# Gate transposes behind the second and third projections, copied by ScalarE; the weight sums' transfers on GpSimd's own queue

## The chip, the cores and the metric

The kernel runs on one core of a Trainium2 chip. The metric is the time of one execution in device microseconds; lower is better. "The profiled execution" is one execution taken by the hardware profiler.

## The reference

One decoder block over 1024 tokens of width 1024, float32. After a root mean square norm, one product with `w_in` gives the inputs of two parallel token mixers: RWKV-7 (r, k, v and three low-rank inputs) and an mLSTM (q, k, v, o and two gates a head). Their outputs go through `w_out`; then comes a gated ConvFFN.

```python
h = rmsnorm(x, norm1_g[l]);  proj = h @ w_in[l]
y_rw = rwkv7_group(p_rw, ...);  y_ml = mlstm_group(p_ml, ...)
x = x + jnp.concatenate([y_rw, y_ml], axis=-1) @ w_out[l]
u = rmsnorm(x, norm2_g[l]) @ w_ffn_up[l];  a, b = u[..., :D_FF], u[..., D_FF:]
x = x + (jax.nn.silu(causal_dwconv(a, ...)) * b) @ w_ffn_down[l]

# mlstm_group, gates of four heads and 1024 tokens
ig = softcap((ig + i_bias).astype(jnp.float32))
logf = jax.nn.log_sigmoid(softcap((fg + f_bias).astype(jnp.float32)))
# in mlstm_chunkwise: b = cumsum(fc), running maxima m_t, and
# h = num / max(|den|, exp(-m_t)), chunk by chunk with a carried state
```

## The kernel before

Tokens lie along the free dimension. Each float32 product is three fp32r matmuls of high and low parts (`mm3`, L211 to L214). The order of the work is written in the program, but a scheduler under it sets each engine's queue and gives tiles of one tag to buffers; a tile that takes a used buffer waits for every user of the tile before it. The tag `slab` has four such buffers.

The stretch of interest begins behind the norm and the mLSTM's value projection (`vgates`). `gates()` turns the gate inputs `gtm` (tokens on partitions) into rows: eight transposes for the input gate and eight for the forget gate (L392), four copies out of PSUM (L394) into the rows `igr` and `lfr` of a `slab` tile (`slab_797`), two scans (L395, L396), differences and exponentials into the rows of a second one (`slab_798`), transposes back (L417), and two copies into `tcol` (L419), which every mLSTM chunk reads.

Then the projections run in the order q0, q1, mk0, mk1, lo, g, r0 to r3, k0 to k3, v0 to v3. `project()` makes two halves of 512 tokens, each 24 matmuls of 128x512. Their weights come by SP's queue (L218); ScalarE casts the high half (L200), GpSimd subtracts the low half (L201). q and mk pass a causal convolution into another `slab` tile (`do_qk`, L460 to L490). The mLSTM's eight chunks run as generators that one `tick()` in each projection advances: scores (L512, L514), values (L532, L537), state (L550, L557), key transposes (L519, L521), normalization (L541 to L565) and the transposes back (L569).

Beside all this, sums and differences of the blocks of `w_down`, needed only by the last product, are made in eleven jobs, each of two 512 KB loads (L306), two subtractions on VectorE (L311, L313) and two on GpSimd (L312, L314), and one 1 MB store (L317). They share one `slab` tile (`slab_671`) used as a ring of two. Before, loads and stores are issued by SP, in one queue with the projections' weights. `next(weight_sums)` and `spawn(weight_sums)` set where they stand.

Of the kernel before, what the change touches and what calls it, by code (L numbers as in the profile page):

```python
# [17 lines left out]
P = 128  # L18
# [55 lines left out]
def block_kernel(ctx, tc, x, wp, wv, pc, rows, brow, lnrow, wud, wug, w_out, wup, w_down, cst, out):  # L74
    nc = tc.nc
    MM = nc.tensor.matmul
    V = nc.vector
    S = nc.scalar
    G = nc.gpsimd
    dma = nc.sync.dma_start  # L80
# [100 lines left out]
    HF = [slice(0, HALF), slice(HALF, T)]  # L181
# [15 lines left out]
    d_w = dram.tile([NP, P, 4, HALF], F32, name="d_w")  # L197
# [99 lines left out]
    wsums = {}  # L297
    ws_slab = []

    def ws_load(p):  # L300

        if not ws_slab:
            ws_slab.append(slab([P, 2, 4, HALF]))
        wsums[p] = b = ws_slab[0][:, p % 2]
        for q in range(2):
            dma(out=b[:, 2 * q:2 * q + 2], in_=w_down[(2 * p + q) * P:(2 * p + q + 1) * P, :].rearrange("p (h t) -> p h t", h=2))  # L306

    def ws_sum(p):

# [4 lines left out]
        G.tensor_tensor(out=b21, in0=b21, in1=b22, op=ALU.subtract)  # L314

    def ws_store(p):
        dma(out=d_w[p], in_=wsums.pop(p))  # L317

    def ws_jobs():

# [41 lines left out]
    tcol = tmp.tile([P, NT, 4, 4], F32, name="tcol")  # L362

    def gates():
# [20 lines left out]
        V.tensor_tensor(out=ga[:, 0, :], in0=ga[:, 0, :], in1=ga[:, 1, :], op=ALU.mult)  # L385
        V.tensor_tensor(out=ga[:, 0, :], in0=ga[:, 0, :], in1=ga[:, 2, :], op=ALU.mult)
        V.scalar_tensor_tensor(out=yf, in0=yf, scalar=0.0, in1=ga[:, 0, :], op0=ALU.min, op1=ALU.subtract)
        for g, dst in ((0, igr), (1, lfr)):
            for hf in range(2):
                ps = bank(3)  # L390
                for t_ in range(4):
                    nc.tensor.transpose(out=ps[0:4, t_ * P:(t_ + 1) * P], in_=gtm[:, g, 4 * hf + t_, :],  # L392
                                        identity=ident)
                V.tensor_copy(out=dst[:, HF[hf]], in_=ps[0:4, :])  # L394
        V.tensor_tensor_scan(out=mr, data0=lfr, data1=igr, initial=0.0, op0=ALU.add, op1=ALU.max)  # L395
        V.tensor_tensor_scan(out=br, data0=rm128, data1=lfr, initial=0.0, op0=ALU.mult, op1=ALU.add)  # L396
        V.tensor_tensor(out=st[0:4, :], in0=igr, in1=br, op=ALU.subtract)
# [13 lines left out]
        V.tensor_tensor(out=lf3, in0=st3[0:4], in1=al3[:, :, P - 1:P].broadcast_to([4, NT, P]), op=ALU.add)  # L411
        S.activation(out=st[64:68, :], in_=lfr, func=AF.Exp)
        S.activation(out=st[96:100, :], in_=mr, func=AF.Exp, scale=-1.0)
        for hf in range(2):
            ps = bank(3)
            for t_ in range(4):
                nc.tensor.transpose(out=ps[:, t_ * P:(t_ + 1) * P], in_=st[:, (4 * hf + t_) * P:(4 * hf + t_ + 1) * P],  # L417
                                    identity=ident)
            V.tensor_copy(out=tcol[:, 4 * hf:4 * hf + 4],  # L419
                          in_=ps.rearrange("p (c q r) -> p c q r", c=4, q=4)[:, :, :, 0:4])  # L420


    active = []
# [21 lines left out]
    def project(name):  # L445
        w = pweights(name)
        ps = [phalf(w, 0, 1)]
        tick()
        ps.append(phalf(w, 1, 2))
        return ps  # L450
# [323 lines left out]
    def do_v2(p, ts):  # L774
# [8 lines left out]
                    in_=t_o.rearrange("p (c e v) -> p e c v", c=4, e=2)[:, e])  # L783
        yield 1

    gates()
    spawn(weight_sums)
    for name in ORDER[:-IN_CHAIN]:
        i = int(name[-1]) if name[-1].isdigit() else 0
        if name[0] == "k":  # L790
            do_k(i)
        else:
            ps = project(name)
            if name[0] == "q":
                do_qk(i, ps)
            elif name[0] == "m":
                do_qk(2 + i, ps)
                if i == 1:
                    spawn(mlstms())
            elif name[0] == "o":  # L800
                for hf in range(2):
                    do_o(i, hf, ps[hf], t2("vt"), t2("lnb"))
            elif name == "lo":
                do_lo(ps)
            elif name == "g":
                do_g(ps)
            elif name[0] == "r":
                do_r(i, ps)
            else:
                do_v(i, ps)  # L810
        tick()
# [469 lines left out]
    with tc.tile_pool(name="ff", bufs=1) as ff:  # L1281
# [182 lines left out]
        for f in range(1, 3):  # L1464
            r = raw_up(f)
# [203 lines left out]
```

## Time and profile before

| | us |
|---|---|
| median of three runs | 1375.9 |
| the three runs | 1374.04, 1375.9, 4844.43 |
| profiled execution | 1363.99 |
| its span | 1362.2 |
| PE busy in the span | 1273.2 (93%) |
| DVE, ACT, POOL busy | 1008.4, 525.0, 508.5 |
| mean granted clock | 0.963 |

A row of a timeline gives an instruction's start, its length, and in brackets the idle time of its engine just before it with what ended that. Matmuls overlap in the pipeline, so a matmul's length is more than the step from one to the next. PEclk 1.00 in a window is TensorE's full clock of 2.4 GHz, 0.50 is 1.2 GHz.

### The profile page before, as it was taken

The page shows a single profiled execution, that of the slowest core. Times are in us where ns is not written, and L with a number is a line of the kernel's source. Part 1 is how long each engine was busy: PE and PEld are TensorE (multiplying, and loading weights), DVE is VectorE, ACT ScalarE, POOL GpSimd, SP SyncE. Part 2 cuts the span into 40 slices and gives each one's busy share as a digit, 9 for nine tenths or more (in the row PEclk, how much of TensorE's full clock was granted, in tenths as well). Part 3 has the DMA queues.
Part 4 walks back from the last instruction along what each step waited for, and adds up shares of the span by engine and source line. Part 5 has one row for each costly group of instructions (what it writes and reads, how often), then busy time and mean ns, then how long its engine had stood idle before and what let it go on. Part 6 is the DMA issues. An engine that isn't in the chain of part 4 may idle for free.

```text
span 1362.2 us, 21298 instructions
## 1 busy us (share of the span) xinstructions
PE 1273.2 (93%) x7814; PEld 1018.1 (75%) x7814; DVE 1008.4 (74%) x1723; ACT 525.0 (39%) x949; POOL 508.5 (37%) x373
## 2 busy tenths in 40 slices
PE   5979999987988999999989999999999997999997
PEld 5967777765866767777767888888888885888886
DVE  6459776699488877777589878778877787567655
ACT  6323432665121233332344333333333334444452
POOL 3533211445244443321374554564456542113000
PEclk9989899999986897999989999999999998999999
DMA  7756232154744566543422333233322329965643
GB/s 276 264 229 229 97 98 81 48 160 115 191 127 115 165 185 185 154 120 102 146 93 86 108 116 105 94 104 105 105 88 98 109 85 342 312 193 188 188 122 124
DMA packets 149816, 199.25 MB, mean 146 GB/s; under 512 B 52168, under 2 KB 90952, under 8 KB 148304
## 3 DMA queue, kind: packets, MB, share of 16 engines
q1 hardware_dynamic: 136400, 180.45, 40.9%
q10 hardware_dynamic: 12032, 13.25, 3.3%
q0 software_dynamic: 1280, 4.20, 1.0%
q8 instruction: 62, 1.02, 0.3%
q14 instruction: 42, 0.34, 0.1%
HBM read 137.25 MB, written 60.59 MB: 145 GB/s over the span
## 4 chain that ended last, share of the span: by engine, by line
PE 40%; DVE 29%; POOL 12%; ACT 7%; DMA 6%; issue 5%; SPq 1%; ACTq 0%; DVEq 0%; POOLq 0%
PE ps L212 10%; PE ps L213 10%; PE ps L214 10%; DVE op L201 6%; POOL raw L1311 4%; DVE f L1308 3%; DVE fu L1308 3%; POOL rw L1311 3%; POOL sl L1311 2%; DMA slab<-in_w_down_dram 2%; DVE f L460 2%; DVE slab L752 2%; POOL rw L1308 2%; DVE slab L754 1%; ACT op L200 1%
## 5 line engine op out<-in xcount | busy, mean ns | idle before, releaser
L212 PE MATMUL ps<-sl,op 128*128 128x512 f32 x572 | 228.3, 399 | 8.5 <-DVE f L1308 6.4
L214 PE MATMUL ps<-sl,op 128*128 128x512 f32 x572 | 226.2, 395 | 0.0
L213 PE MATMUL ps<-sl,op 128*128 128x512 f32 x572 | 225.5, 394 | 0.3 <-DVE op L201 0.3
L212 PE MATMUL ps<-sl,w 128*128 128x512 f32 x416 | 173.9, 418 | 0.0
L214 PE MATMUL ps<-sl,w 128*128 128x512 f32 x416 | 168.0, 404 | 0.0
L213 PE MATMUL ps<-sl,w 128*128 128x512 f32 x416 | 167.9, 404 | 0.0
L1311 POOL TENSOR_TENSOR raw<-raw,rw 128x512 f32<-128x512 f32 x44 | 90.2, 2051 | 164.8 <-DVE op L201 160.9
L213 PE MATMUL ps<-slab,op 128*128 128x512 f32 x352 | 139.5, 396 | 3.5 <-DVE op L201 3.5
L212 PE MATMUL ps<-slab,op 128*128 128x512 f32 x352 | 140.2, 398 | 1.6 <-ACT op L200 0.8
L214 PE MATMUL ps<-slab,op 128*128 128x512 f32 x352 | 139.5, 396 | 0.0
L212 PEld LDWEIGHTS ps<-sl,op 128*128 128x128 f32 x572 | 108.0, 189 | 36.4 <-DVE f L1308 6.8
L214 PEld LDWEIGHTS ps<-sl,op 128*128 128x128 f32 x572 | 108.4, 189 | 25.8
L213 PEld LDWEIGHTS ps<-sl,op 128*128 128x128 f32 x572 | 108.6, 190 | 25.3 <-DVE op L201 0.7
L201 DVE TENSOR_TENSOR op<-rw,op 128x512 fp32r<-128x512 f32 x69 | 72.7, 1054 | 64.4 <-ACT op L200 63.1
L201 DVE TENSOR_TENSOR op<-slab,op 128x512 fp32r<-128x512 f32 x75 | 58.1, 774 | 69.5 <-ACT op L200 69.4
L200 ACT CAST op<-rw 128x512 fp32r<-128x512 f32 x69 | 42.5, 619 | 155.9 <-POOL rw L1311 79.3
L201 POOL TENSOR_TENSOR w<-raw,w 128x1024 fp32r<-128x1024 f32 x22 | 55.2, 2508 | 116.7 <-ACT w L200 114.6
L212 PEld LDWEIGHTS ps<-sl,w 128*128 128x128 f32 x416 | 80.3, 193 | 18.3 <-issue 1.1
L214 PEld LDWEIGHTS ps<-sl,w 128*128 128x128 f32 x416 | 80.0, 192 | 17.7 <-issue 0.2
L213 PEld LDWEIGHTS ps<-sl,w 128*128 128x128 f32 x416 | 80.5, 194 | 16.2 <-issue 0.9
L200 ACT CAST op<-slab 128x512 fp32r<-128x512 f32 x75 | 46.5, 620 | 94.2 <-PE ps L214 64.4
L213 PEld LDWEIGHTS ps<-slab,op 128*128 128x128 f32 x352 | 67.0, 190 | 19.9 <-DVE op L201 4.5
(315 smaller groups left out, 2656.4 us busy)
## 6 DMA issues: line engine op xcount, KB each, us to landing
slab<-d_go SPq DMA_DIRECT2D x75, 256.0 KB, 4.1
raw<-in_wup_dram SPq DMA_DIRECT2D x23, 512.0 KB, 3.2
rw<-in_wup_dram SPq DMA_DIRECT2D x23, 512.0 KB, 4.1
slab<-in_w_down_dram SPq DMA_DIRECT2D x22, 512.0 KB, 5.8
raw<-in_wp_dram SPq DMA_DIRECT2D x22, 512.0 KB, 4.6
d_w<-slab SPq DMA_DIRECT2D x11, 1024.0 KB, 4.4
d_go<-sl SPq DMA_DIRECT2D x44, 256.0 KB, 2.0
slab<-d_w SPq DMA_DIRECT2D x44, 256.0 KB, 4.5
```

The costliest lines, as they stand in the source:

```text
L200: S.copy(out=h, in_=src)
L201: (leng or V).tensor_tensor(out=l, in0=src, in1=h.bitcast(F32), op=ALU.subtract)
L212: MM(out=ps, lhsT=ah, rhs=bl, start=start, stop=False)
L213: MM(out=ps, lhsT=al, rhs=bh, start=False, stop=False)
L214: MM(out=ps, lhsT=ah, rhs=bh, start=False, stop=stop)
L460: V.scalar_tensor_tensor(out=out[:, sh:HALF], in0=ps[hf][:, 0:HALF - sh], scalar=scal, in1=out[:, sh:HALF], op0=ALU.mult, op1=ALU.add)
L752: V.tensor_tensor(out=tv, in0=wv_[:, s_:s_ + 1, s_ + 1:32].broadcast_to([P, n, m]), in1=wv_[:, 0:n, s_:s_ + 1].broadcast_to([P, n, m]), op ...
L754: V.tensor_tensor(out=wv_[:, 0:n, s_ + 1:32], in0=wv_[:, 0:n, s_ + 1:32], in1=tv, op=ALU.add)
L1308: eng.tensor_tensor(out=o, in0=a, in1=b, op=ALU.add)
L1311: eng.tensor_tensor(out=o, in0=a, in1=b, op=ALU.subtract)
```

## The change

The weight sums' loads and stores are issued by GpSimd. `gates()` becomes a generator of three pieces, of which the second (transposes into rows, scans) is run behind q1's two halves and the third (transposes back) behind mk0's; the six copies out of PSUM go to ScalarE. Line numbers behind the change are 1 to 6 above those of before (L394 is L395 there, L417 is L419, L512 is L515, L532 is L535).

```diff
--- before.py
+++ after.py
@@ -303,7 +303,7 @@
             ws_slab.append(slab([P, 2, 4, HALF]))
         wsums[p] = b = ws_slab[0][:, p % 2]
         for q in range(2):
-            dma(out=b[:, 2 * q:2 * q + 2], in_=w_down[(2 * p + q) * P:(2 * p + q + 1) * P, :].rearrange("p (h t) -> p h t", h=2))
+            G.dma_start(out=b[:, 2 * q:2 * q + 2], in_=w_down[(2 * p + q) * P:(2 * p + q + 1) * P, :].rearrange("p (h t) -> p h t", h=2))
 
     def ws_sum(p):
 
@@ -314,7 +314,7 @@
         G.tensor_tensor(out=b21, in0=b21, in1=b22, op=ALU.subtract)
 
     def ws_store(p):
-        dma(out=d_w[p], in_=wsums.pop(p))
+        G.dma_start(out=d_w[p], in_=wsums.pop(p))
 
     def ws_jobs():
 
@@ -385,13 +385,14 @@
         V.tensor_tensor(out=ga[:, 0, :], in0=ga[:, 0, :], in1=ga[:, 1, :], op=ALU.mult)
         V.tensor_tensor(out=ga[:, 0, :], in0=ga[:, 0, :], in1=ga[:, 2, :], op=ALU.mult)
         V.scalar_tensor_tensor(out=yf, in0=yf, scalar=0.0, in1=ga[:, 0, :], op0=ALU.min, op1=ALU.subtract)
+        yield
         for g, dst in ((0, igr), (1, lfr)):
             for hf in range(2):
                 ps = bank(3)
                 for t_ in range(4):
                     nc.tensor.transpose(out=ps[0:4, t_ * P:(t_ + 1) * P], in_=gtm[:, g, 4 * hf + t_, :],
                                         identity=ident)
-                V.tensor_copy(out=dst[:, HF[hf]], in_=ps[0:4, :])
+                S.copy(out=dst[:, HF[hf]], in_=ps[0:4, :])
         V.tensor_tensor_scan(out=mr, data0=lfr, data1=igr, initial=0.0, op0=ALU.add, op1=ALU.max)
         V.tensor_tensor_scan(out=br, data0=rm128, data1=lfr, initial=0.0, op0=ALU.mult, op1=ALU.add)
         V.tensor_tensor(out=st[0:4, :], in0=igr, in1=br, op=ALU.subtract)
@@ -411,13 +412,15 @@
         V.tensor_tensor(out=lf3, in0=st3[0:4], in1=al3[:, :, P - 1:P].broadcast_to([4, NT, P]), op=ALU.add)
         S.activation(out=st[64:68, :], in_=lfr, func=AF.Exp)
         S.activation(out=st[96:100, :], in_=mr, func=AF.Exp, scale=-1.0)
+        yield
         for hf in range(2):
             ps = bank(3)
             for t_ in range(4):
                 nc.tensor.transpose(out=ps[:, t_ * P:(t_ + 1) * P], in_=st[:, (4 * hf + t_) * P:(4 * hf + t_ + 1) * P],
                                     identity=ident)
-            V.tensor_copy(out=tcol[:, 4 * hf:4 * hf + 4],
-                          in_=ps.rearrange("p (c q r) -> p c q r", c=4, q=4)[:, :, :, 0:4])
+            S.copy(out=tcol[:, 4 * hf:4 * hf + 4],
+                   in_=ps.rearrange("p (c q r) -> p c q r", c=4, q=4)[:, :, :, 0:4])
+        yield
 
 
     active = []
@@ -783,7 +786,8 @@
                     in_=t_o.rearrange("p (c e v) -> p e c v", c=4, e=2)[:, e])
         yield 1
 
-    gates()
+    gate_steps = gates()
+    next(gate_steps)
     spawn(weight_sums)
     for name in ORDER[:-IN_CHAIN]:
         i = int(name[-1]) if name[-1].isdigit() else 0
@@ -791,6 +795,8 @@
             do_k(i)
         else:
             ps = project(name)
+            if name in ("q1", "mk0"):
+                next(gate_steps)
             if name[0] == "q":
                 do_qk(i, ps)
             elif name[0] == "m":
```

The program gives the scheduler this order, and the scheduler sets queues and buffers anew. From about r3 on, every engine's queue is the same as before. Three places differ.

VectorE before, the copies of the forget gate's rows (`slab_797`) between the weight sums' subtractions (`slab_671`):

```order
L387 SCALAR_TENSOR_TENSOR gtm<-gtm,q_99_804 128x32 [waits DVE_49]
L311 TENSOR_TENSOR slab_671<-slab_671 128x512 [waits DMAHW6_49,DMAHW1_49]
L394 COPY slab_797<-ps_827 4x512 [waits PE_49]
L394 COPY slab_797<-ps_833 4x512 [waits PE_49]
L460 SCALAR_TENSOR_TENSOR uv_921<-ps_865,pc_68,uv_921 128x511 [waits Activation_49]
L395 SCALAR_TENSOR_TENSOR slab_797<-slab_797 4x1024 [waits DVE_49]
```

The same copies in the change, now on ScalarE, with the casts of the low-rank input (`vt`, `row`) ahead of them and the cast of r0's weights (`w_226`) behind (`ps_969` and `ps_975` are the forget gate's transposes):

```order
L602 CAST row_156_1289<-uv_1290 64x512 [waits Activation_49]
L395 COPY slab_797<-ps_957 4x512 [waits DMASW4_49,DMASW3_49,DMASW5_49,DMASW2_49,DMASW6_49,DMASW1_49,DMASW7_49,DMASW0_49,Pool_49]
L395 COPY slab_797<-ps_963 4x512
L472 ACTIVATE uv_1301<-ps_1264,pc_68 128x512 [waits PE_49]
L395 COPY slab_797<-ps_969 4x512 [waits PE_49]
L395 COPY slab_797<-ps_975 4x512 [waits PE_49]
L200 CAST w_226_1625<-raw_1623 128x1024 [waits DMAHW7_49]
L597 ACTIVATE uv_1301<-uv_1301 64x512 [waits DVE_49,Activation_49]
```

The gate rows stand in the buffer that was the weight sums' ring: the first copy waits for the ring's transfers on all of GpSimd's DMA semaphores and for GpSimd itself, where the copies of before waited for a transpose alone.

TensorE in the change, the end of lo's projection and the start of g's (weights `w_180`, `w_181`):

```order
L213 MATMUL ps_1264<-sl_3_88,w_147_1208 128x512
L214 MATMUL ps_1264<-sl_3_88,w_146_1207 128x512
L393 MATMUL ps_969<-cs,gtm 4x128 [waits PE_49,Activation_49]
L393 MATMUL ps_969<-cs,gtm 4x128 x3
L393 MATMUL ps_975<-cs,gtm 4x128 [waits PE_49,Activation_49]
L393 MATMUL ps_975<-cs,gtm 4x128 x3
L212 MATMUL ps_1387<-sl_2_87,w_180_1383 128x512
L213 MATMUL ps_1387<-sl_1_86,w_181_1384 128x512 [waits Pool_49]
```

The forget gate's transposes, which in the kernel before stand two matmuls into q0's second half, stand right ahead of g, and wait for ScalarE's copies. The transposes back (L417 before, in q1's second half) have moved three matmuls into r0, and the chunks follow them, here with r0's weights (`w_226`, `w_227`):

```order
L419 MATMUL ps_1081<-cs,slab_798 128x128 [waits PE_49,Activation_49]
L419 MATMUL ps_1081<-cs,slab_798 128x128 x3
L419 MATMUL ps_1087<-cs,slab_798 128x128 [waits PE_49]
L419 MATMUL ps_1087<-cs,slab_798 128x128 x3
L212 MATMUL ps_1629<-sl_2_87,w_226_1625 128x512
L213 MATMUL ps_1629<-sl_1_86,w_227_1626 128x512
L214 MATMUL ps_1629<-sl_1_86,w_226_1625 128x512
L515 MATMUL ps_1251<-slab_868 128x128 [waits Activation_49]
L515 MATMUL ps_1252<-slab_868 128x128 [waits Activation_49]
L515 MATMUL ps_1251<-slab_868 128x128
L515 MATMUL ps_1252<-slab_868 128x128
L553 MATMUL ps_1331<-slab_117,q_154_1262 64x129 [waits DVE_49]
```

All eight mLSTM chunks stand from here to r3's first half; before, the first began between lo's two halves and the others came one in each half projection.

GpSimd in the change, the last part of the weight sums (`w_147` is lo's weights, `w_181` is g's):

```order
L317 DMA d_w<-slab_671 128x2048 [waits Pool_49]
L201 TENSOR_TENSOR w_147_1208<-raw_1205,w_146_1207 128x1024 [waits DMAHW5_49,PE_49,Activation_49]
L312 TENSOR_TENSOR slab_671<-slab_671 128x512 [waits DMASW3_49,DMASW2_49,DVE_49]
L306 DMA slab_671<-in_w_down_dram 128x1024 [waits DMASW4_49]
L314 TENSOR_TENSOR slab_671<-slab_671 128x512 [waits DVE_49]
L306 DMA slab_671<-in_w_down_dram 128x1024
L317 DMA d_w<-slab_671 128x2048 [waits Pool_49]
L201 TENSOR_TENSOR w_181_1384<-raw_1381,w_180_1383 128x1024 [waits DMAHW6_49,PE_49,Activation_49]
L312 TENSOR_TENSOR slab_671<-slab_671 128x512 [waits DMASW6_49,DMASW5_49,DVE_49]
L314 TENSOR_TENSOR slab_671<-slab_671 128x512 [waits DVE_49]
L317 DMA d_w<-slab_671 128x2048 [waits Pool_49]
```

Before, GpSimd held L312, L314 and L201 alone. Now the loads and stores stand between them, each in line with the subtractions, and the last store (of the eleventh sum) stands behind the low half of g's weights.

## Rows read from the trace of the kernel before

**Rows 1.** The page: busy time of each engine over the span.

```profile
PE 1273.2 (93%) x7814; PEld 1018.1 (75%) x7814; DVE 1008.4 (74%) x1723; ACT 525.0 (39%) x949; POOL 508.5 (37%) x373
```

**Rows 2.** Windows: stretch, its length, busy us per engine, PEclk, DMA share, GB/s.

```profile
83.40:90.50 7.10, 0.05 (x1) 0.00 (x0) 5.27 (x11) 0.22 (x1) 2.52 (x2) 0.81 0.69 279
90.50:94.50 4.00, 3.96 (x14) 2.92 (x15) 3.23 (x5) 0.55 (x1) 1.26 (x1) 0.50 0.65 266
148.00:152.60 4.60, 2.03 (x11) 1.42 (x10) 3.86 (x11) 2.76 (x4) 2.33 (x1) 1.00 0.23 62
152.60:159.40 6.80, 6.80 (x18) 4.89 (x18) 6.09 (x23) 3.67 (x8) 0.03 (x1) 0.50 0.23 77
159.40:243.40 84.00, 81.72 (x475) 64.70 (x474) 57.45 (x214) 27.07 (x53) 12.81 (x8) 1.00 0.30 86
165.10:207.00 41.90, 40.50 (x250) 31.88 (x250) 32.70 (x125) 15.05 (x31) 5.38 (x3) 1.00 0.35 100
```

**Rows 3.** TensorE timeline: start us, us, line, tile, idle before and its releaser.

```profile
90.54 1.87 PE L392 MATMUL ps<-cs,gtm 128*4 128x128 f32 x8 [7.09 <-DVE gtm L387]
...
109.05 1.06 PE L417 MATMUL ps<-cs,slab 128*128 128x128 f32 x8 [1.95 <-issue]
...
111.12 0.39 PE L213 MATMUL ps<-sl,w 128*128 128x512 f32 x1
...
126.99 0.39 PE L214 MATMUL ps<-sl,w 128*128 128x512 f32 x1
```

**Rows 4.** TensorE timeline: chunk 0, g's first matmul, first wait, first matmul of k0.

```profile
139.54 0.71 PE L512 MATMUL ps<-slab 64*128 64x128 f32 x8
...
145.98 1.27 PE L532 MATMUL ps<-slab,TT 128*128 128x129 f32 x8
...
147.96 0.48 PE L212 MATMUL ps<-sl,w 128*128 128x512 f32 x1
...
151.24 0.68 PE L512 MATMUL ps<-slab 64*128 64x128 f32 x4 [2.57 <-DVE bt L545]
...
243.24 0.62 PE L641 MATMUL ps<-row,lnb 128*128 128x512 f32 x2
```

**Rows 5.** VectorE timeline: last gate copy and the first scan.

```profile
92.45 0.68 DVE L394 COPY slab<-ps 4x512 f32<-4x512 f32 x1 [0.17 <-PE ps L392]
...
93.71 2.27 DVE L395 TENSOR_TENSOR_SCAN slab<-slab 4x1024 f32<-4x1024 f32 x1
```

**Rows 6.** SyncE queue timeline: loads and stores of the weight sums.

```profile
94.67 0.80 SPq L306 DMA_DIRECT2D slab<-in_w_down_dram  x2
...
111.06 0.34 SPq L317 DMA_DIRECT2D d_w<-slab  x1
...
130.08 0.88 SPq L306 DMA_DIRECT2D slab<-in_w_down_dram  x2
...
143.29 0.33 SPq L317 DMA_DIRECT2D d_w<-slab  x1
```

**Rows 7.** GpSimd timeline around the last sum.

```profile
139.44 2.58 POOL L201 TENSOR_TENSOR w<-raw,w 128x1024 fp32r<-128x1024 f32 x1 [0.97 <-ACT w L200]
...
141.98 1.29 POOL L314 TENSOR_TENSOR slab<-slab 128x512 f32<-128x512 f32 x1
```

**Rows 8.** The page, DMA issues: count, KB each, median us to landing.

```profile
slab<-in_w_down_dram SPq DMA_DIRECT2D x22, 512.0 KB, 5.8
...
d_w<-slab SPq DMA_DIRECT2D x11, 1024.0 KB, 4.4
```

**Rows 9.** Tile d_hml: transfers that GpSimd issues in the kernel before.

```profile
L580 POOL DMA_DIRECT2D row<-d_hml x7: 538/543/729, 311.7 to 492.3; - x7
...
DMA to landing us min/median/max: 2.3/4.7/6.2
```

**Rows 10.** VectorE lines, 165.1 to 207 us (four chunks): busy us, mean ns.

```profile
L514 DVE SCALAR_TENSOR_TENSOR TT<-ps,TT 128x256 f32<-128x256 f32 x8 | 3.4, 420 | 0.6 <-PE ps L512 0.5
...
L460 DVE SCALAR_TENSOR_TENSOR slab<-ps,pcs,slab 128x511 f32<-128x511 f32 x3 | 2.2, 745 | 1.9 <-ACT slab L469 1.9
```

## The prediction

> **What bounds the kernel now.** The page comes first: TensorE is busy for 1273.2 of 1362.2 us [rows 1], so time can be won or lost where it stands, and where its clock falls behind a stand. From about r3 on the queues of before and of the change are the same on all engines; so only the stretch up to the first matmul of k0, at 243.24 us [rows 4], can move the end, and what k0 starts later by, the kernel ends later by. I went through that stretch by windows and by TensorE's timeline. The largest stand is 83.4 to 90.5 us: the forget gate's transposes wait 7.09 us for the gate values that VectorE ends late [rows 2, 3]. Behind it the clock is granted at 0.50 for 4.0 us, which costs half of that, 2.0 us [rows 2]. The transposes back wait 1.95 us [rows 3]. The mLSTM's chunks then cost a wait of 2.57 us ahead of chunk 1 [rows 4], 6.8 us at 0.50, 3.4 lost, and 84.0 − 81.7 = 2.3 us of idle in 159.4 to 243.4 [rows 2]. These are the whole of what the change could win here: about 19 us.
>
> SP's queue shows the weight sums: last loads at 130.08, last store at 143.29 [rows 6], landed some 4.4 us later [rows 8], at 147.7. TensorE begins g at 147.96 [rows 4]. In the kernel before nothing but the last product waits for that store.
>
> **The change part by part.** *The copies on ScalarE* cost TensorE nothing by themselves; six copies of about 0.7 us (VectorE's is 0.68 [rows 5]; none on ScalarE in that shape is in the trace, and half or double moves the end by 1 us) go to an engine that is 39% busy [rows 1].
>
> *The buffer of the gate rows* is what decides. In the change the first copy waits until the ring of the weight sums is through: all loads, subtractions and the last store's landing. Behind it on ScalarE wait the other copies, the second half of lo and the cast of r0's weights; behind the copies wait the forget gate's transposes, and behind those, on TensorE, g and all that follows. So g starts when the last store has landed, and not when TensorE is free.
>
> When is that? The ring is two deep, and each round goes store, load, landing, four subtractions; its landings and subtractions are as before. Did SP's queue hold it up? The last store was issued as soon as GpSimd's last subtraction ended (141.98 + 1.29 = 143.27, store at 143.29 [rows 6, 7]), so SP added nothing there, and I give no gain for leaving SP. GpSimd's issue of one transfer takes 0.54 us where it issues others in this kernel [rows 9], SP's about 0.33 for a store and 0.40 for a load (0.80 for two) [rows 6]. A round has one store and two loads in its chain, 3 × 0.54 = 1.6 against 1.1 us, and the subtractions and low halves of weights now stand in one queue with them, so I double it: 0.8 to 1 us a round over the four rounds that are left behind 94.67 us, +4. The last store then goes at 147 and lands 4.4 us later, at about 151.5. Two copies of 0.7 us and the eight transposes (1.87 us at the low clock [rows 3], which is what TensorE has after such a stand) put g's first matmul at 155, **+7.0 us** against 147.96. This takes in the stalls that go (7.09, 1.95 and 2.0): TensorE does q0 to lo sooner and waits longer ahead of g. It also takes in the waits for the low halves of weights, which now queue behind loads and stores on GpSimd (2 or 3 us each at mk0, mk1 and lo, no end of the sum as long as the ring ends later). A half projection is 24 steps of 0.227 us (71 matmuls from 111.12 to 126.99 [rows 3]), 5.45 us: TensorE could be ready for g at about 137 to 145.
>
> *Work moved behind g.* Chunk 0's scores, values and state (0.65 + 1.98 us by starts, of which the part that moves is 2.6 [rows 4]) and the transposes back (109.05 to the next matmul, 0.8 us [rows 3]) lay ahead of g and now lie behind: **+3.4 us**.
>
> *The wait of the transposes back.* From the end of the last gate copy (92.45 + 0.68 = 93.13) to their start at 109.05 [rows 3, 5] the chain of scans and exponentials took 15.9 us. Now the last copy ends at about 156, so they can start at 172. TensorE has for cover the two halves of g and three matmuls, 10.9 + 0.7 us from 155: 166.6. That leaves **+5.2 us**; a low clock in g only eats from it.
>
> *Eight chunks in six halves.* Before, each half projection had one chunk. Over four of them (165.1 to 207.0) TensorE was busy 40.5 of 41.9 us and VectorE 32.7 [rows 2]: 8.2 us of VectorE a chunk, and on TensorE 10.1, of which 4.7 are the chunk's. In the change the chunks stand from r0's first half to r2's second, the last transposes in r3: 6 × 5.45 + 8 × 4.7 = 70 us of TensorE, and VectorE has 8 × 8.2 = 65 us in it, 93% where it was 78%. The values' matmuls stand one to six matmuls (0.2 to 1.4 us) behind the scores', and between them VectorE has two products of 0.42 us [rows 10], beside mixing products of 0.75 us that it may be in [rows 10]. I take 1 us of wait a chunk, 8 us, and for the tail of the last chunk, which no other chunk covers, half of its 8.2 us and a hop, 5 us: 13 us, an estimate between 3 us (the tail partly covered, nothing else) and 25 us (three times the wait per chunk and none covered). Before, the waits and the low clock here took 2.57 + 2.3 + 3.4 = 8.3 us. So **+4.8 us**, with ends of −5 and +17.
>
> *The clock.* Behind the stand ahead of g, and again behind the waits among the chunks, I expect the low clock once more than counted: 6.8 us at 0.50 as in 152.6 to 159.4 [rows 2], **+3.4 us**, between 0 and 7.
>
> The sum is 7.0 + 3.4 + 5.2 + 4.8 + 3.4 = 23.8 us. On the profiled execution that is 1364.0 + 23.8 = 1388; that execution lies 12 us under the median of the runs shown, and against the median it is 1375.9 + 24 = **1400 us**, +1.7%. About 2%, 27.5 us, is what a measurement of this kernel can tell from no change; so the forecast is "within", near its upper edge.
>
> **Rivals.** *GpSimd's queue is slow* (slower, beyond 2%). If GpSimd can start the transfers only when VectorE is between instructions, each issue is late by up to one VectorE instruction, 0.7 us (products, copies) to 2.27 us (scans [rows 5]); three in a round's chain and five rounds make 10 to 34 us. It decides as soon as the last store goes later than about 150 us; taken at 16 us, g starts at 171 and the end is 1400 + 16 = 1416. For it: VectorE is busy most of this stretch (5.27 of 7.10 us at 83.4 to 90.5 [rows 2]). Against it: GpSimd issues transfers elsewhere in 538 to 729 ns, which land in 2.3 to 6.2 us, with a VectorE that is 74% busy over the span [rows 1, 9]. Chance 0.20. The Trainium skill states such a rule ("SBUF — State Buffer", section "A bandwidth-pool intuition that's wrong (but worth ruling out)"): a transfer issued by GpSimd took about 3100 ns instead of 620 where a VectorE copy ran beside it, since GpSimd could not write its descriptors. By these figures, as an estimate, 33 transfers late by 2.5 us each would come to 80 us if all of them met a copy. The trace's transfers from GpSimd (543 ns the median issue [rows 9]) don't agree with that, though they stand in another stage.
>
> *The ring is done early* (no change). If loads that no longer stand behind SP's weight loads pull the ring ahead, so that the last store has landed by 137, only the removed stalls count: g at about 147.96 − 7.1 − 2.0 − 1.95 − 2.6 = 134 to 137, which is 12.5 less in the middle, then 3.4 + 5.2 + 4.8 more: +1, between 1372 and 1381, taken at 1377. For it: from 94.67 to 130.08 the ring took 17.7 us a round [rows 6], and a store, a load and four subtractions of 1.3 us are 4.4 + 5.8 + 5.2 = 15.4 [rows 7, 8]. Against it: the last store left at once behind its subtraction [rows 6, 7], so the ring waits for transfers and subtractions and not for SP. Chance 0.14.
>
> *The chunks are covered* (no change). The ring holds g up as forecast, but VectorE keeps up with the denser chunks at the lower end (3 us of waits), and the clock does not fall again: 24 − 10 − 3 = 11, 1387 us. Chance 0.16.
>
> That the change doesn't do what it says can be left out: it does; the queue shows both copies and transfers moved.
>
> **How the numbers follow.** The forecast has 0.50, between 1391 and 1412 by the ends of its terms that are independent (the chunks' 8 us and the ring's 4 us either way). Beyond 1403.4 (+2%) lies two fifths of that, 0.20, and nearly all of the slow queue, 0.19: slower 0.39. Faster by 2% would need 1348, 27.5 us less, and all stalls here together are 19: 0.02, for what I don't see. Within 2%: 0.59. The range of 8 in 10 goes from 1376 (leaving out the lower half of the early ring) to 1424 (leaving out the upper part of the slow queue).
>
> **What would show it.** Right: no stand of 7 us at 83 us; g's first matmul at 151 to 158 us with a stand of at least 8 us ahead of it (the transposes L393 of `ps_969` included), released by ScalarE; L395's first copy starting within 1 us of the landing of the eleventh store; a wait of 2 to 6 us at L419; k0's first matmul at 260 to 272 us; low clock behind the stands. Wrong: L317's last issue before 137 or after 152 us, GpSimd's issues much over 0.6 us, the first copy running long before the last landing, or TensorE's stretch behind k0 differing from before by more than 5 us.

## The result and the profile after

The change takes 1387.8 us (median of four runs) against 1375.2 for the kernel before; the ratio of their runs on record is 1.014, 95% interval [1.010, 1.018], which is 14 to 24 us more. By the means of the runs that are listed with it (before without the one of 4844 us) it is less, 1.010. The 83 runs of before that were taken beside the experiments have means of 1366.9, 1370.7 and 1368.5 us, and against these the change's mean of 1388.4 is 1.3 to 1.6% more. The profiled execution took 1388.6 us, span 1386.9, against 1362.2.

TensorE first, by windows (stretch, length, busy us of PE, PEld, DVE, ACT, POOL, then PEclk, DMA share, GB/s):

```profile
76.00:99.00 23.00, 23.00 (x110) 19.08 (x109) 7.92 (x20) 4.60 (x8) 10.86 (x15) 1.00 0.69 255
...
99.00:128.00 29.00, 25.81 (x109) 20.33 (x108) 21.75 (x32) 10.68 (x14) 15.21 (x14) 0.94 0.62 226
...
147.00:153.50 6.50, 0.50 (x4) 0.08 (x3) 3.83 (x5) 3.19 (x7) 1.84 (x2) 0.88 0.40 165
...
153.50:160.00 6.50, 6.50 (x22) 4.93 (x23) 4.83 (x4) 5.23 (x8) 3.00 (x1) 0.59 0.01 4
...
171.30:262.30 91.00, 83.25 (x481) 63.48 (x482) 61.15 (x243) 29.67 (x65) 12.04 (x7) 0.94 0.33 92
```

The stand of 7.1 us at 83 us [rows 2] is gone: from 76 to 99 us TensorE is never idle. The loss comes later. The 6.5 us ahead of 153.5 hold 0.5 us of work, the 6.5 behind them run at 0.59, and from 171.3 on 7.8 of 91 us are idle. TensorE's table of waits from 76 us up to k0 tells who ended these waits, and shorter ones between 99 and 147 us (line, releaser: us in total, times, longest):

```profile
PE ps L393 <- ACT slab L395: 6.0, 1, 6.0
...
PE ps L213 <- POOL w L201: 5.9, 3, 3.6
...
PE ps L572 <- DVE bt L568: 2.9, 3, 2.3
...
PE ps L419 <- ACT slab L413: 2.7, 1, 2.7
...
PE ps L535 <- DVE TT L517: 2.2, 2, 1.7
...
PE ps L515 <- DVE ty L171: 1.8, 1, 1.8
```

The timeline at the three places of the forecast: ahead of g, the transposes back, k0.

```profile
153.49 1.87 PE L393 MATMUL ps<-cs,gtm 128*4 128x128 f32 x8 [6.00 <-ACT slab L395]
...
155.00 0.78 PE L212 MATMUL ps<-sl,w 128*128 128x512 f32 x1
...
171.32 1.09 PE L419 MATMUL ps<-cs,slab 128*128 128x128 f32 x8 [2.70 <-ACT slab L413]
```

```profile
262.39 0.62 PE L644 MATMUL ps<-row,lnb 128*128 128x512 f32 x2
```

g begins at 155.0 (147.96 before [rows 4]) and k0 at 262.4 (243.24): 19.2 us later. On ScalarE and GpSimd, the last store and the first gate copies:

```profile
141.91 2.42 POOL L201 TENSOR_TENSOR w<-raw,w 128x1024 fp32r<-128x1024 f32 x1 [2.56 <-ACT w L200]
...
148.63 0.58 POOL L317 DMA_DIRECT2D d_w<-slab  x1 [0.30 <-POOL slab L314]
```

```profile
152.86 1.05 ACT L395 COPY slab<-ps 4x512 f32<-4x512 f32 x2 [1.25 <-issue]
...
155.39 0.57 ACT L395 COPY slab<-ps 4x512 f32<-4x512 f32 x1 [0.28 <-PE ps L393]
```

The profile names no releaser for the first copy (`issue`), but the store's landing can be read by itself:

```profile
L317 POOL DMA_DIRECT2D d_w<-slab x1: 576/576/576, 148.6 to 148.6; - x1
...
DMA to landing us min/median/max: 4.2/4.2/4.2
```

The store is issued at 148.63 and lands 4.2 us later, at 152.8; the first copy starts at 152.86, and 0.6 us later the transposes. So the gate rows do wait for the ring, as the queue of ScalarE says.

**k0's start is the better gauge.** Behind k0 the queues of TensorE, VectorE and ScalarE are the same in all fourteen kernels of this study, and yet the profiled time from k0's first matmul to the end goes from 1116.0 to 1129.4 us among them. It is 1119.0 in the profile of before and 1124.5 in that of the change; these 5.5 us lie within that scatter. The runs' ratio (+1.4%, 19 us, between 14 and 24) has the 19.2 us at k0 in its middle and the 24.7 between the two profiles just outside. So I read each experiment at k0 and by its ratio. Each k0 is one execution, and how far it moves from execution to execution was not measured; where k0 and ratio disagree, the ratio is the one that stands on several runs.

| kernel | k0's first matmul, us | against before | ratio to before, 95% interval |
|---|---|---|---|
| before | 243.2 | | |
| the change | 262.4 | +19.2 | 1.014 [1.010, 1.018] |
| e1 queue only | 257.8 | +14.6 | 1.013 [1.010, 1.016] |
| e2 gates only | 244.9 | +1.7 | 1.004 [1.001, 1.007] |
| e3 change, gate rows in one slab | 249.2 | +6.0 | 1.002 [1.000, 1.005] |
| e5 e3 with SP's queue | 240.8 | −2.4 | 0.999 [0.996, 1.003] |
| e6 stores alone on GpSimd | 249.7 | +6.5 | 1.004 [1.002, 1.007] |
| e7 loads alone on GpSimd | 250.6 | +7.4 | 0.999 [0.995, 1.002] |
| e8 e5, other banks, third piece later | 242.4 | −0.8 | 1.000 [0.998, 1.003] |
| e9 e5 with VectorE's copies | 239.0 | −4.2 | 0.997 [0.994, 1.000] |
| e10 e1, first two sums on SP | 251.4 | +8.2 | 1.004 [1.000, 1.007] |
| e11 change, first two sums on SP | 263.7 | +20.5 | 1.014 [1.010, 1.018] |
| e12 before, all subtractions on GpSimd | 249.4 | +6.2 | 1.006 [1.002, 1.009] |
| e13 e9, all subtractions on GpSimd | 252.0 | +8.8 | 1.008 [1.005, 1.011] |

The ratio of e7 leaves out four of its ten runs (1380.1 to 1383.1 us) as slow, since they lie more than 1.5% above its fastest, 1356.2 us; the means over all ten give 1.002.

### The profile page after: what moved, and what is told of

The parts are those of the page before. It is cut to its first block, busy times and chain, and to the rows that moved or that the text cites. A ratio compares the mean times of both kernels' runs of the same rounds, so it can differ in the third digit from the quotient of the medians.

```text
span 1386.9 us, 21292 instructions
## 1 busy us (share of the span) xinstructions
PE 1284.2 (93%) x7814; PEld 1024.1 (74%) x7814; DVE 1004.3 (72%) x1717; ACT 527.0 (38%) x955; POOL 524.9 (38%) x406
## 4 chain that ended last, share of the span: by engine, by line
PE 27%; DVE 17%; POOL 11%; ACT 4%; issue 3%; DMA 2%; SPq 0%; ACTq 0%; DVEq 0%; POOLq 0%
PE ps L212 7%; PE ps L214 7%; PE ps L213 7%; DVE op L201 6%; POOL raw L1317 4%; DVE f L1314 3%; DVE fu L1314 2%; POOL rw L1317 2%; POOL sl L1317 2%; DVE f L463 2%; POOL rw L1314 2%; ACT op L200 1%; ACT f L1407 1%; POOL sl L1314 1%; DVE slab L201 1%
## 5 line engine op out<-in xcount | busy, mean ns | idle before, releaser
L213 PE MATMUL ps<-sl,w 128*128 128x512 f32 x416 | 171.9, 413 | 5.9 <-POOL w L201 5.9
L212 PE MATMUL ps<-sl,w 128*128 128x512 f32 x416 | 176.2, 424 | 0.9 <-ACT w L200 0.9
L214 PE MATMUL ps<-sl,w 128*128 128x512 f32 x416 | 171.5, 412 | 0.0
L201 DVE TENSOR_TENSOR op<-rw,op 128x512 fp32r<-128x512 f32 x69 | 72.7, 1055 | 66.9 <-ACT op L200 65.7
L201 DVE TENSOR_TENSOR op<-slab,op 128x512 fp32r<-128x512 f32 x75 | 58.3, 777 | 68.9 <-ACT op L200 64.5
L201 POOL TENSOR_TENSOR w<-raw,w 128x1024 fp32r<-128x1024 f32 x22 | 54.8, 2489 | 120.7 <-ACT w L200 91.9
L213 PEld LDWEIGHTS ps<-sl,w 128*128 128x128 f32 x416 | 81.9, 197 | 24.1 <-POOL w L201 7.2
L212 PEld LDWEIGHTS ps<-sl,w 128*128 128x128 f32 x416 | 81.8, 197 | 19.9 <-ACT w L200 1.2
L214 PEld LDWEIGHTS ps<-sl,w 128*128 128x128 f32 x416 | 81.9, 197 | 17.9 <-issue 0.6
```

The source lines that it names most:

```text
L201: (leng or V).tensor_tensor(out=l, in0=src, in1=h.bitcast(F32), op=ALU.subtract)
L212: MM(out=ps, lhsT=ah, rhs=bl, start=start, stop=False)
L213: MM(out=ps, lhsT=al, rhs=bh, start=False, stop=False)
L214: MM(out=ps, lhsT=ah, rhs=bh, start=False, stop=stop)
```

## The experiments

**Two parts apart, and with the ring's wait taken away (e1, e2, e3, e5).** e1 and e2 each have one part of the change. In e3 the gates need one slab: the second tile's two free rows hold `lfr` and `igr`, `br` overwrites `rm128` and `mr` stands in `st`'s first rows until it is used, so that no row takes the ring's buffer. e5 is e3 with SP's queue.

```diff
 e1 (on before), and the reverse in e2 and e5 (on the change, on e3)
-            dma(out=b[:, 2 * q:2 * q + 2], in_=w_down...)
+            G.dma_start(out=b[:, 2 * q:2 * q + 2], in_=w_down...)
-        dma(out=d_w[p], in_=wsums.pop(p))
+        G.dma_start(out=d_w[p], in_=wsums.pop(p))
 e3 (on the change)
-        rt = slab([P, 4, T])
-        lfr, igr, mr, br = (rt[0:4, i, :] for i in range(4))
+        rm128, lfr, igr = (rt2[0:4, i, :] for i in (1, 2, 3))
+        mr, br = st[0:4, :], rm128
...
+        S.activation(out=st[96:100, :], in_=mr, func=AF.Exp, scale=-1.0)
+        al = lfr
```

Expected of e1: 

> Kernel before, with only the weight sums' loads and stores moved to GpSimd's queue; gates as before, so no copy waits for the ring. Theory A (the price is the gate rows' buffer, which has to wait for the ring): no stand of 10 us anywhere ahead of g; L392's wait of 7.1 us stays; one or two waits of 2 to 4 us for low halves of weights on GpSimd; k0 at 241 to 249 us (before 243.2), time within 0.6% of before. Rival B (GpSimd's queue is the price): k0 at 258 us or later, time 1 to 2% above before.

Expected of e2: 

> The change without its queue part: gates in three pieces with ScalarE's copies, weight sums on SP as before. Theory A: the first copy waits for the ring here too, and the forget gate's transposes, which stand inside mk1 here, start only when the last store has landed, at 145 to 150 us, after a stand of 15 us or more on TensorE; k0 at 255 to 262 us, time 0.8 to 1.5% above before. Rival B: without GpSimd's transfers the ring is done earlier, no long stand, k0 at 230 to 240 us, time 0.3 to 1% below before.

Expected of e3: 

> The whole change, but the gates' rows need one slab instead of two: the second tile's free rows hold them, with two of them in place, so no row waits for the ring's buffer. Theory A: the stand of 6.0 us ahead of g and the wait at L419 are gone, the chunks come one in each half projection again, k0 at 232 to 243 us, time 0 to 0.9% below before (the 7.1 us stand of before is gone, GpSimd's waits for weights of up to 6 us stay). Rival B (queue): k0 stays at 255 us or later.

Expected of e5: 

> As the run with one slab for the gates' rows, but the weight sums on SP's queue as in the kernel before: only the gates' move and ScalarE's copies, without the ring's wait. Theory A: no wait for low halves behind transfers on GpSimd; k0 at 230 to 236 us, 0.5 to 1% below before, 2 to 6 us earlier than with GpSimd's queue. Rival C (queue gains by itself, since SP's order no longer holds weights up): k0 later than with GpSimd's queue.

Theory A, mine, fell for e1: the queue alone costs 14.6 of the 19.2 us, with nobody waiting for the ring's buffer. For e3 it had the direction and not the size (6.0 above before where 0 to 11 below was expected; the rival's 255 us was not reached either). e2 (244.9) came earlier than it said, and e5 (240.8) later than its 230 to 236, though rival C is out, since k0 is earlier than in e3. The four read as a square, at k0: the ring's wait costs 244.9 − 240.8 = 4.1 us with SP's queue, and 262.4 − 249.2 = 13.2 with GpSimd's; the queue costs 8.4 us without that wait (e5 to e3) and 17.5 with it (e2 to the change). The gates' move by itself is worth 2.4. These are differences of single executions. By the ratios the same four prices are about 6, 16, 4 and 13 us, so the shape of the square holds; but e3 and e5 can't be told from before by theirs, so neither the 6.0 nor the 2.4 is shown by itself.

e2 shows why. Its last store, on SP's queue, and the copy and the transposes that wait for it:

```profile
126.49 0.33 SPq L317 DMA_DIRECT2D d_w<-slab  x1
```

```profile
130.97 1.05 ACT L395 COPY slab<-ps 4x512 f32<-4x512 f32 x2 [0.59 <-DMA d_w<-slab]
```

```profile
131.59 1.87 PE L393 MATMUL ps<-cs,gtm 128*4 128x128 f32 x8 [11.49 <-ACT slab L395]
```

126.5 us, against 143.29 before [rows 6] and 148.6 in the change: with the gates moved, and their scans out of the way of VectorE's subtractions, the ring ends 17 us sooner, and GpSimd's queue makes it 22 us later again. The other pair agrees: in e1 the last store goes at 162.9, 20 us later than before, and 14 later than in the change. The stand at the transposes is 11.5 us long but lies in mk1, with chunks still spread.

In e1 VectorE shows the loss (start, length, instruction, idle before it):

```profile
81.94 0.69 DVE L311 TENSOR_TENSOR slab<-slab 128x512 f32<-128x512 f32 x1 [8.20 <-DMA slab<-in_w_down_dram]
...
84.68 0.69 DVE L311 TENSOR_TENSOR slab<-slab 128x512 f32<-128x512 f32 x1 [1.91 <-DMA slab<-in_w_down_dram]
...
89.65 1.00 DVE L375 TENSOR_SCALAR gtm<-gtm 128x64 f32<-128x64 f32 x1 [0.32 <-ACT gtm L374]
```

L375, the gates' first operation on VectorE, stands behind subtractions that wait for loads. In the kernel before the same two subtractions ran at 70.29 and 73.72 and L375 at 78.59. TensorE's stand at L392 grows to 9.85 us (ahead of the input gate's transposes now), but the transposes back start at 114.4, only 5.3 us later than before. The larger part of the loss comes behind them, where the wait for chunk 1 grows from 2.57 [rows 4] to 8.5. VectorE stands there behind the eleventh sum, whose load GpSimd issued late:

```profile
150.02 0.53 POOL L306 DMA_DIRECT2D slab<-in_w_down_dram  x1
158.77 1.26 POOL L312 TENSOR_TENSOR slab<-slab 128x512 f32<-128x512 f32 x1 [8.21 <-DMA slab<-in_w_down_dram]
```

```profile
160.06 0.69 DVE L313 TENSOR_TENSOR slab<-slab 128x512 f32<-128x512 f32 x1 [5.80 <-POOL slab L312]
```

```profile
164.33 1.19 PE L512 MATMUL ps<-slab 64*128 64x128 f32 x4 [8.51 <-DVE bt L545]
```

The lateness starts on GpSimd, in the change and in e1 alike; of the change:

```profile
30.84 3.39 POOL L244 TENSOR_TENSOR slab<-raw,slab 128x1040 fp32r<-128x1040 f32 x1
...
34.17 1.61 POOL L306 DMA_DIRECT2D slab<-in_w_down_dram  x3
...
44.22 2.39 POOL L201 TENSOR_TENSOR w<-raw,w 128x1024 fp32r<-128x1024 f32 x1
...
46.55 0.58 POOL L317 DMA_DIRECT2D d_w<-slab  x1
```

Three of the first four loads stand behind L244 (the split of the mLSTM's weights), the first store behind L201: 34.2 and 46.6 us, where SP issued the last two of those loads from 30.2 on and the store at 37.2:

```profile
30.21 0.91 SPq L306 DMA_DIRECT2D slab<-in_w_down_dram  x2
...
37.21 0.33 SPq L317 DMA_DIRECT2D d_w<-slab  x1
```

It goes on from there. A load that takes a buffer has to wait until the store of the buffer's last sum has landed, and on GpSimd everything behind it in the queue waits too. In the change these waits are 16.5 us; on SP, in the kernel before, the same line waits 13.1 us and no subtraction stands behind it:

```profile
POOL slab L306 <- DMA d_w<-slab: 16.5, 6, 6.1
```

**Loads or stores (e6, e7).** One of the two lines of e1 each.

Expected of e6: 

> Kernel before, with only the eleven stores of the weight sums on GpSimd's queue, loads on SP. A store follows its own last subtraction on GpSimd and never waits there for a transfer. Theory D (the queue costs because GpSimd stands in line for landings: a load that waits until a store has landed holds up the subtractions behind it): no wait of L306 on GpSimd, k0 at 240 to 247 us (before 243.2), time within 0.4% of before. Rival E (transfers started by GpSimd are slow by themselves, to issue or to land): k0 4 us or more later, stores landing over 6 us.

Expected of e7: 

> Kernel before, with only the 22 loads of the weight sums on GpSimd's queue, stores on SP. Theory D: L306 waits on GpSimd for landings of stores, 10 us or more in all, VectorE's subtractions wait for the loads and hold the gate chain up; the stand ahead of the forget gate's transposes is longer than 7.1 us, and k0 comes at 250 to 258 us (257.8 with both on GpSimd), 0.5 to 1.3% above before. Rival E: k0 between those of before and of both together by the share of the transfers, 22 of 33, about 253, with issue times of L306 over 0.8 us or landings over 7 us.

Theory D missed in e6 (249.7 where it said 240 to 247). In e7 it had the waits for landings (12.0 us on GpSimd) and k0 (250.6), but not the time: the ratio does not tell e7 from before, and over all ten runs it is 1.002. At k0 the two parts add up (6.5 + 7.4 = 13.9, together 14.6), by the ratios they don't, so that the sum is not shown. Rival E's two signs for e6 were met: k0 is 6.5 us later, and the stores landed in a median 6.7 us, against 4.4 before [rows 8]. Seven of the eleven took 6.0 to 7.9 us, all of them issued while a load of the other sum was under way; the other four took 4.2 to 5.0. So they are slower beside other transfers, and what that is worth at k0 no run separates. In the change the loads land in a median 5.2 us (5.8 before), the stores in 5.2, and in e7 the loads in 5.6; no issue took more than 0.71 us.

What e1, e6 and e7 have in common is that L375 comes at 89.7 to 92.8 us, behind a subtraction that waits for its load: by a late start in e1, by queue order in e6 (the subtractions keep the pace of before, the sixth L311 at 74.38, but the scheduler put two more sums ahead of L375), by both in e7. That alone does not give the size of the loss, as the later points show (us; e10 is the next experiment):

| kernel | L375 | transposes back | wait ahead of chunk 1 | last store issued | k0 |
|---|---|---|---|---|---|
| before | 78.6 | 109.1 | 2.6 | 143.3 | 243.2 |
| e1 | 89.7 | 114.4 | 8.5 | 162.9 | 257.8 |
| e6 | 90.7 | 119.2 | 1.6 | 141.2 | 249.7 |
| e7 | 92.8 | 119.5 | 0.2 | 138.0 | 250.6 |
| e10 | 89.4 | 113.2 | 2.6 | 151.3 | 251.4 |

With loads or stores alone on GpSimd the ring ends no later than before, and chunk 1 waits no longer. With both it ends 20 us later, and its last sum holds up chunk 1.

**The late start taken away (e10, e11).**

```diff
-            G.dma_start(out=b[:, 2 * q:2 * q + 2], in_=w_down...)
+            (dma if p < 2 else G.dma_start)(out=b[:, 2 * q:2 * q + 2], in_=w_down...)
-        G.dma_start(out=d_w[p], in_=wsums.pop(p))
+        (dma if p < 2 else G.dma_start)(out=d_w[p], in_=wsums.pop(p))
```

Expected of e10: 

> The run with only the queue moved (weight sums' transfers on GpSimd), but the first two of the eleven sums keep SP for their loads and stores; the other nine stay with GpSimd. Theory H (the loss is a late start: on GpSimd the first loads stand behind the splits of the mLSTM's weights, L244, and the first store behind a low half of weights, L201, so every later sum is 10 us late, and VectorE's subtractions, which wait for them, hold the gate chain up): the fifth L311 comes at 68 to 74 us instead of 81.9, L375 at 77 to 83 instead of 89.7, k0 at 243 to 249 us (257.8), time within 0.5% of before. Theory D (the waits for landings within GpSimd's queue, all along): k0 at 254 us or later, 0.8% or more above before.

Expected of e11: 

> The whole change, but the first two of the eleven weight sums keep SP's queue. Theory H: the last store goes 8 to 12 us earlier than 148.6, ScalarE's first gate copy starts at 141 to 147 us instead of 152.9, the stand ahead of it on TensorE does not grow, k0 at 251 to 257 us (262.4), 0.4 to 0.9% below the change. Theory D: the last store at 146 us or later, k0 at 260 us or later.

In e10 the fifth subtraction is back at 71.0, as theory H says, and 6.4 of e1's 14.6 us come back. What comes back is the wait ahead of chunk 1, which is 2.57 us as before. The rest stays: the scheduler set one more sum ahead of L375, whose subtraction waits at 88.14, and L375 comes at 89.36:

```profile
85.48 0.69 DVE L311 TENSOR_TENSOR slab<-slab 128x512 f32<-128x512 f32 x1 [8.01 <-DMA slab<-in_w_down_dram]
...
88.14 0.69 DVE L311 TENSOR_TENSOR slab<-slab 128x512 f32<-128x512 f32 x1 [1.83 <-DMA slab<-in_w_down_dram]
...
89.36 0.19 DVE L375 TENSOR_SCALAR gtm<-gtm 128x64 f32<-128x64 f32 x1
```

In e11 the last store goes 4.5 us earlier, at 144.1, and the first copy at 148.5, between the two theories; k0 does not come earlier. The forget gate's transposes there stand 19 matmuls into lo's first half instead of behind lo, so that less work lies ahead of the stand (8.9 us long instead of 6.0) and 29 matmuls (6.6 us) more behind it. An earlier end of the ring was spent on that. Since the order changed with it, the run does not tell what the late start alone costs the whole change. Of the 22 us by which GpSimd's queue moves the last store, the earlier start gives back 4.5 here. For the rest the waits for landings and the places behind L201 are left, and no run takes those away.

**The waiting subtraction (e12, e13).** All four subtractions on GpSimd.

```diff
-        V.tensor_tensor(out=b11, in0=b12, in1=b11, op=ALU.subtract)
+        G.tensor_tensor(out=b11, in0=b12, in1=b11, op=ALU.subtract)
...
-        V.tensor_tensor(out=b22, in0=b22, in1=b11, op=ALU.subtract)
+        G.tensor_tensor(out=b22, in0=b22, in1=b11, op=ALU.subtract)
```

Expected of e12: 

> Kernel before, with all four subtractions of each weight sum on GpSimd, none on VectorE; transfers on SP. If VectorE's subtractions that wait for loads are what holds the gates up: L375 at 77 to 79 us, L387 at 84 us or before (90.2 in the kernel before), the stand of 7.1 us at L392 at most 2 us; GpSimd has 22 times 1.3 us more and delays low halves of weights by up to 3 us once or twice; k0 at 233 to 239 us, 0.3 to 0.8% below before. Rival: GpSimd becomes the wait of TensorE (L201), k0 at 243 us or later.

Expected of e13: 

> The best so far (gates' rows in one slab, transfers on SP, copies on VectorE, gates in three pieces), with all four subtractions of each weight sum on GpSimd. If the 7.9 us stand at L392 there is VectorE's lateness behind waiting subtractions: it falls to 3 us or less, k0 at 229 to 235 us against 239.0, time 0.6 to 1.1% below before. Rival: the low halves on GpSimd become the wait, k0 at 239 us or later.

The stand at L392 falls from 7.1 to 1.7 us in e12 and goes in e13: VectorE's waiting subtractions are what made most of it. But in both the rival was right, GpSimd is the next bound:

```profile
85.41 1.03 PE L392 MATMUL ps<-cs,gtm 128*4 128x128 f32 x8 [1.71 <-DVE gtm L387]
...
105.93 1.94 PE L417 MATMUL ps<-cs,slab 128*128 128x128 f32 x8 [5.64 <-POOL slab L314]
...
128.56 0.79 PE L213 MATMUL ps<-sl,w 128*128 128x512 f32 x1 [5.01 <-POOL w L201]
```

```profile
PE ps L213 <- POOL w L201: 16.2, 3, 6.4
```

In e13 TensorE waits 16.2 us for three low halves of weights.

**A better version (e8, e9).** On e5:

```diff
 e8
-                ps = bank(3)
+                ps = bank(3 + g)
-            if name in ("q1", "mk0"):
+            if name in ("q1", "mk1"):
 e9
-                S.copy(out=dst[:, HF[hf]], in_=ps[0:4, :])
+                V.tensor_copy(out=dst[:, HF[hf]], in_=ps[0:4, :])
...
-            S.copy(out=tcol[:, 4 * hf:4 * hf + 4], ...
+            V.tensor_copy(out=tcol[:, 4 * hf:4 * hf + 4], ...
```

Expected of e8: 

> The run with one slab for the gates' rows and the weight sums on SP, and two changes: the forget gate's transposes go to other PSUM buffers than the input gate's (bank 4), so that they need not wait for ScalarE's copies, and the third piece of the gates stands behind mk1 instead of mk0. If the stands of 7.3 us at L392 and 2.7 us at L419 there are all of the loss: both gone, with up to 2 to 3 us of low clock; k0 at 228 to 233 us against 240.8, time 0.6 to 1.0% below before. Rival: the stand only moves to the chunks (their first needs the same columns), k0 at 238 us or later.

Expected of e9: 

> The run with one slab for the gates' rows and the weight sums on SP, but with the six copies on VectorE as in the kernel before. Theory F (ScalarE's copies cost by their place: they stand behind the convolution's activations, which wait for VectorE): the stand at L392 is 3 us or less instead of 7.3, k0 at 233 to 238 us. Rival G (the engine of the copies is all one): k0 within 2 us of 240.8.

The stand only moved in e8: 5.9 us ahead of a projection that waits for VectorE's convolution (L467), and 3.6 for ScalarE's `tcol` at chunk 0. In e9 it stayed (first row e5, second e9), and its releaser is VectorE's copy instead of ScalarE's:

```profile
107.20 1.01 PE L392 MATMUL ps<-cs,gtm 128*4 128x128 f32 x4 [7.31 <-ACT slab L394]
```

```profile
108.17 1.01 PE L392 MATMUL ps<-cs,gtm 128*4 128x128 f32 x4 [7.90 <-DVE slab L394]
```

So the copies' engine is nearly all one (1.8 us at k0), theory G. e9 is the fastest kernel measured, 0.997 [0.994, 1.000] of before, an interval that all but touches 1: about 4 us by k0 and by the ratio, between 1 and 8 by its interval, and no more can be claimed.

## Why the prediction came out, and which of its steps did not

- **Time.** 1400 was forecast, 1388 measured, within the range; +1.7% forecast, +1.4% measured. The sum was 4.6 us too large (23.8 against 19.2 at k0), by two errors behind g that partly cancel: waits 8 us too high, low clock 3 us too low (below). The medians of the runs listed lie 12.6 us apart, the ratio's interval holds 19.
- **The ring releases g: right, its 7.0 us in part by luck.** The store lands at 152.8 (151.5 forecast) and g starts at 155.0 (155), because the transposes follow the first copy by 0.6 us and not two copies later. The landing took the 4.2 us that the median of 4.4 made likely; that of the last store before took 6.4. The stand ahead of g is 6.0 us where I had asked for at least 8: that sign is missed, since TensorE was through with lo at 147.5, and I had it ready at 137 to 145.
- **Why the ring ends then: wrong.** "SP added nothing there, and I give no gain for leaving SP", and landings and subtractions "as before": the last store was to go 4 us later, at 147, by issue times alone. It went at 148.6 by two larger effects that nearly cancel, which is luck: the gates' move lets the ring end at 126.5 (e2), and GpSimd's queue costs 22 us. The mistake was to price the queue by its issues (0.2 us each more) and not by what they stand behind. I listed what waits behind a transfer on GpSimd, and not what a transfer waits behind. Nor did I look at what leaves VectorE.
- **"The buffer … is what decides": half right.** Without its wait the change still costs 6.0 us at k0 (e3; its ratio of 1.002 shows less), and with it but without the queue 1.7 (e2). With the gates moved, the wait needs the queue for most of its price, and the queue the wait for half of its own; with the gates left in place the queue alone costs 14.6 (e1).
- **The slow queue: the rival's mechanism did not show in the issues.** No issue of L306 or L317 took more than 0.71 us, over 33 transfers beside a VectorE that was 75% busy from 99 to 128 us:

```profile
L306 POOL DMA_DIRECT2D slab<-in_w_down_dram x22: 527/532/708, 18.9 to 138.2; - x22
...
L317 POOL DMA_DIRECT2D d_w<-slab x11: 538/576/578, 46.6 to 148.6; - x11
```

  The rule cited from the Trainium skill ("SBUF — State Buffer", "A bandwidth-pool intuition that's wrong (but worth ruling out)") gives the time of a whole transfer, beside a copy on VectorE. So the landings are what to hold against it, and those of the change (median 5.2 us for loads and for stores, 5.8 and 4.4 before) are not 2.5 us longer each. But of the 82 us that VectorE was busy beside these transfers, copies were 0.7, so the rule is not seen here, and not tested either. Stores do land later from GpSimd (median 5.2 us here, 6.7 in e6), so it is not shown that the order in the queue is all of its price. The 2.3 to 6.2 us of landing that the prediction read from [rows 9] take in eight transfers of SP on the same tile; the eight of GpSimd land in 3.0 to 6.2.
- **Waits for weights on GpSimd: right in size** (5.9 us in three). As said, they are covered by the ring's wait in the change.
- **The transposes back.** 5.2 us of wait forecast, starting at 172; it started at 171.3 after 2.7 us, and the low clock behind the stand ([rows 2]'s 6.8 us at 0.50; here 6.5 at 0.59) ate the rest, as the text allowed.
- **The chunks: mis-sized.** 13 us of waits were forecast; from 171.3 us on 7.8 us of idle came, the largest piece 2.3 us at the last transposes back (L572). The order of instructions was close, and VectorE followed the chunks more closely than the 1 us a chunk that I had taken. The upper end of the term does not follow from its words: three times the wait per chunk and an uncovered tail are 24 + 8 = 32 us, not 25.
- **The clock: mis-sized.** 3.4 us were forecast. TensorE's busy time from g's start to k0 grew by 6.5 us, of which 3.4 are the work moved; the other 3.1, about, come on top of the 3.4 that the low clock cost before, so some 6.5 in all (before, then the change):

```profile
147.96:243.24 95.28, 90.44 (x500) 70.89 (x500) 67.40 (x245) 33.37 (x65) 15.16 (x9) 0.96 0.30 85
```

```profile
155.00:262.39 107.39, 96.97 (x534) 74.32 (x533) 75.16 (x256) 37.56 (x76) 16.56 (x9) 0.93 0.30 84
```

- **The sign that I set as wrong** (over 5 us behind k0) is met, 5.5, and is scatter, as the tails of the other kernels show.

## What to carry to other kernels

A transfer that moves to a computing engine's queue has to be priced in both directions: what it holds up, and what it now stands behind, from the first one on. Where a scheduler gives out buffers and order, moving a step later can give its tile another buffer; read in the new queue what the first writer waits for. And compare two kernels at the last point where their queues differ: here one start time differs by 6 us where whole runs don't tell two kernels apart. But a start time is one execution; take it from several before you claim it.

## What was not expected of the hardware

- The same queues from k0 on took from 1116.0 to 1129.4 us in fourteen profiled executions. What makes the difference stays open.
- In e1 a product of VectorE (L505, both inputs in SBUF; its mean in the stretch of [rows 10] is 0.69 us) took 4.00 us from 121.11 on, while GpSimd ran L201 (120.87, 2.44 us) and L314 (123.28, 1.27 us), and ended half a us behind the latter:

```profile
121.11 4.00 DVE L505 TENSOR_TENSOR TT<-TT,cs 128x512 f32<-128x512 f32 x1
```

```profile
120.87 2.44 POOL L201 TENSOR_TENSOR w<-raw,w 128x1024 fp32r<-128x1024 f32 x1
...
123.28 1.27 POOL L314 TENSOR_TENSOR slab<-slab 128x512 f32<-128x512 f32 x1
```

  The Trainium skill ("SBUF — State Buffer", "Who interferes with whom") says that a VectorE instruction with two SBUF inputs contends with a GpSimd instruction that reads SBUF, and that the second to start waits. These rows agree with it as far as L201 goes; the product also outlasts L314, which started 2.2 us behind it. In the kernel before the same line took 2.48 us from 113.86 on, beside L201 alone (113.35, 2.43 us). No run here isolates it.
